# A hybrid decoder trunk: sliding-window scores folded into one 128x128 block per head, and the running sums of both rates from four products

## The chip, the cores and the metric

One core of a Trainium2 chip. Five engines run their own instruction queues in order and meet by semaphores: TensorE (PE, with its weight loads as PEld), VectorE (DVE), ScalarE (ACT), GpSimd (POOL) and SyncE (SP, which here only issues loads). The metric is the device time of one execution in microseconds (us).

## The reference, cut to what matters

Two layers over 256 tokens of width 1024. Each layer normalises the stream, projects it once, runs three token mixers beside each other, gates and merges them, and adds the result to the stream.

```python
proj = einsum('bsd,de->bse', rms_norm(x, norm_w), w_in)
y_a = mamba2_branch(...)           # running sum of dt * a per head, over 128-token chunks
y_b = sliding_window_branch(...)   # 16 query heads, 4 key heads, window 128, a sink logit per head
y_c = forgetting_attention_branch(...)  # running sum of log_sigmoid(f) per head over all 256 tokens
x = x + einsum(merged, w_out)
...
diff = qi + blk - sj                       # qi: query in its block of 128, sj: key in two blocks
band = (diff >= 0) & (diff < SWA_WINDOW)   # window 128
scores = where(band & (key_pos >= 0), scores, -inf)
probs = softmax(concatenate([scores, sink]))[..., :-1]
```

With a window of 128 and blocks of 128, a query at place i of its block sees keys 0..i of its own block and keys i+1..127 of the block before: two triangles that fill one 128x128 square. The first block has no block before it.

## The kernel before, in words

All products of the stream with weights are made in fp32 out of rounded pieces: ScalarE writes the rounded weights (`hi`, L291), VectorE the rest (`lo`, L292), and TensorE multiplies both. SyncE loads the weights; `feed` and `release` (from L404) keep a few split pieces ahead of TensorE, and a piece that TensorE has used frees the place for the next one. So the splits on ScalarE and VectorE are paced by TensorE, and run some us ahead of it.

TensorE's order is fixed by a planner in the file (L100 to L175): each step of work adds its own cost to a clock, and helper tasks (attention, scan, norms) are generators that `yield` a delay after which `pump` may put their next piece between the dense products. The constants at L25 to L33 are these delays (`D_SOFT` behind the softmax, `D_SOFT2` between two batches of transposes, `D_EVAC` behind the evictions, `D_CUM` behind the rates). The order on VectorE, ScalarE and GpSimd is made by a scheduler that knows the tiles.

PSUM has eight banks. Three of them (`pmm`, tag `mm`) take the dense products; five (`pmx`, tag `mx`, L78) are a rotating pool for all that is small: scores, transposes, products with values, running sums, scan products, norm sums. In the pool each request is a tile of its own of one bank.

`attn_quad` (L593) handles four heads. It is used by eight quads of the sliding window (four in each layer, `swa_quad`, L686) and eight of the forgetting attention (`fox_quad`, L976). Its steps: (1) scores of four heads into four `mx` banks, in each 128 columns for the first block of queries and 256 for the second; (2) for each head and block one VectorE instruction that adds a mask or bias, scales and takes the row's minimum (L615), and one ScalarE exponential with its row sum (L621); the sink's share of the sum (L625 to L628); the reciprocal (L630) and the scaling (L633); (3) after `D_SOFT`, twelve 128x128 transposes on TensorE through three `mx` banks (L650), each bank copied out by ScalarE (L652); six of them, then `D_SOFT2`, then six; (4) later, for two quads at once, the products with the values and the gate (`values`, L673, the multiplications at L676).

`decay_logits` (L714) works out the two rates, 16 heads each, and after `D_CUM` their running sums: two products for `acum` (tokens on partitions), two for the scan's rate and three for the forgetting rate (heads on partitions), in three `mx` banks, then one write to DRAM (`cumd`), from which later steps read rows broadcast to all partitions.

`ssd_group` (L805, four in each layer) transposes its inputs through two `mx` banks (L815), each read by VectorE (L817), makes decay blocks (L830, L832), multiplies them by one bank of products (L845) and puts the scan's products into another bank (L851 to L858). `group_norm` (L902) uses `mx` for row sums and scales (L909, L940). The transposes of the stream between layers (`to_hT`, `mT`) use it too.

Of the kernel before, what the change touches and what calls it, by code (L numbers as in the profile page):

```python
# [16 lines left out]
P = 128  # L17
# [30 lines left out]
def hybrid_trunk(  # L48
# [28 lines left out]

    def pmx():  # L78
        return PS("mx", 5)
# [105 lines left out]
    for j in range(2):  # L185
# [17 lines left out]
    wmask = T("wmask", [P, 2 * P])  # L203
    nc.gpsimd.memset(wmask, 0.0)
    nc.gpsimd.affine_select(out=wmask[:, P:2 * P], in_=wmask[:, P:2 * P],
                            compare_op=ALU.is_ge, fill=NEG, base=0,
                            pattern=[[-1, P]], channel_multiplier=1)
    nc.gpsimd.affine_select(out=wmask[:, 0:P], in_=wmask[:, 0:P],
                            compare_op=ALU.is_ge, fill=NEG, base=-1,
                            pattern=[[1, P]], channel_multiplier=-1)  # L210
# [376 lines left out]
    def attn_quad(y, last, products, biases, nsink, v, vcols, sz, gated, scored=lambda: None):  # L587
# [14 lines left out]
        scs = [pmx() for _ in range(4)]  # L602

        def score(p, i, b):
            return scs[2 * p + i][:, b * P:P + 2 * P * b]

        products(score)
        for p in range(2):
            pp = pps[p]
            ps_ = slice(4 * p, 4 * p + 4)  # L610
            ns = None if nsink is None else nsink(p)
            for i in range(2):
                for b, sl in blocks:
                    e = 4 * p + 2 * i + b
                    nc.vector.tensor_tensor_reduce(  # L615
                        out=pp[:, i, sl], in0=score(p, i, b), in1=biases(p, i, b), scale=-0.125,
                        scalar=1.0e30 if ns is None else ns[:, i:i + 1],
                        op0=ALU.add, op1=ALU.min, accum_out=nm[:, e:e + 1])
                for b, sl in blocks:
                    e = 4 * p + 2 * i + b  # L620
                    act(pp[:, i, sl], pp[:, i, sl], AF.Exp, scale=-1.0, bias=nm[:, e:e + 1],  # L621
                        accum_out=sums[:, e:e + 1])
            if nsink is not None:
                es = T("es", [P, 4], bufs=2)
                tt(es.rearrange("p (i b) -> p i b", i=2), nm[:, ps_].rearrange("p (i b) -> p i b", i=2),  # L625
                   bc(ns, 2, 2), op=ALU.subtract)
                act(es, es, AF.Exp)
                tt(sums[:, ps_], sums[:, ps_], es, op=ALU.add)  # L628
            rs = T("rsum", [P, 4], bufs=4)
            nc.vector.reciprocal(rs, sums[:, ps_])  # L630
            for i in range(2):
                for b, sl in blocks:
                    ts(pp[:, i, sl], pp[:, i, sl], rs[:, 2 * i + b:2 * i + b + 1], 0.5,  # L633
                       op0=ALU.mult, op1=ALU.mult)
        yield D_SOFT
        scored()

        order = [(0, 0), (0, 1), (1, 0), (1, 1), (0, 2), (1, 2),
                 (2, 0), (2, 1), (2, 2), (3, 0), (3, 1), (3, 2)]
        at = {hb: (n // 4, n % 4 * P) for n, hb in enumerate(order)}  # L640
        pTs = []
        for n, (h, b) in enumerate(order):
            if n == 6:
                yield D_SOFT2
            if n % 4 == 0:
                pt = pmx()
            transpose(pt[:, n % 4 * P:(n % 4 + 1) * P], pps[h // 2][:, h % 2, b * P:(b + 1) * P], ident)
            if n % 4 == 3:
                if n == 3:
                    two = T("L4", [P, 2, 512])  # L650
                pT = T("L2", [P, 512]) if n == 11 else two[:, n // 4, :]
                act(pT, pt, AF.Copy)  # L652
                pTs.append(pT)
# [3 lines left out]
        def products_with_values(bank):  # L657
            py = bank()
            for p in range(2):
                for b, o in ((0, 0), (1, P)):  # L660
                    for i in range(2):
                        n, c = at[2 * p + i, 2 * b]
                        mm(py[64 * i:64 * i + 64, S * p + o:S * p + S], v[:, b, vcols(p, i)],
                           pTs[n][:, c:c + S - o], start=(b == 0), stop=(b == 1))
            return py
# [3 lines left out]
        if len(pair) == 2:  # L669
            quads = pair[:]  # L670
            pair.clear()

            def values():  # L673
                for py, (_, _, own) in zip([f(bank) for (_, f, _), bank in zip(quads, (pmx, pmm))], quads):
                    o = own()
                    tt(o, py.rearrange("p (u s) -> p u s", u=2), o, op=ALU.mult)  # L676
            if not last:
                y.values.append(None)
            gates = lambda: all(g() for g, _, _ in quads)
            yield Half(gates) if last else gates  # L680
            if last:
                values()
            else:
                y.values[0] = values

    def swa_quad(y, g, q):  # L686
        yield lambda: 1 in y.sz

        def products(score):
# [8 lines left out]
            y, g == 3, products, lambda p, i, b: wmask[:, P:2 * P] if b == 0 else wmask,  # L698
            lambda p: y.nsink[:, 4 * g + 2 * p:4 * g + 2 * p + 2], y.bv,
            lambda p, i: slice(64 * g, 64 * g + 64),  # L700
            lambda: y.sz[1][:, 2 * g:2 * g + 2, :], lambda: (1, 2 * g + 1) in y.zdone)
# [12 lines left out]
    def decay_logits(y):  # L714
# [21 lines left out]
        lf = T("lf", [P, 2, 16])  # L736
# [5 lines left out]
        ts(lf, lf, 2.0, None, op0=ALU.mult)  # L742
        da = T("da", [P, 2, 16])
        tt(da, y.dt, bc(y.nega, 1, 2), op=ALU.mult)
# [15 lines left out]
        mm(pf[0:16, P:S], lf[:, 1, :], tri, start=False, stop=True)  # L760
        act(cum[:, 1, :], pf[0:16, 0:S], AF.Copy, scale=-8.0)
        y.cumd = dr.tile([16, 2, S], F32, name=f"cumd{y.l}", tag=f"cumd{y.l}")
        nc.scalar.dma_start(y.cumd, cum)
# [40 lines left out]
    def ssd_group(y, g):  # L804
# [3 lines left out]
        nc.scalar.dma_start(bcg, y.cumd[4 * g:4 * g + 4, 0, :].partition_broadcast(P))  # L808
# [169 lines left out]
    def fox_quad(y, j):  # L978
# [3 lines left out]
        for p in range(2):  # L982
            bias = T("bias", [P, 2, 3 * P])
            nc.scalar.dma_start(bias[:, :, P:3 * P],
                                y.cumd[2 * (j + p):2 * (j + p) + 2, 1, :].partition_broadcast(P))
# [528 lines left out]
```

## Time and profile before

| | before |
|---|---|
| median of 3 runs | 820.89 us (820.74 to 822.0) |
| the profiled execution, its own time | 820.72 us |
| its span, first to last instruction | 819.0 us |
| DVE, ACT and POOL busy | 671.5, 547.6 and 172.6 us |
| TensorE records | 5242 matmuls, 5242 weight loads |
| HBM read | 154.63 MB, 191 GB/s over the span |

The page gives busy time by engine, a row of digits for 40 slices of the span, the chain of work that ended last (followed back from the last instruction to what released each step) and groups of instructions, written as out<-in by tile names. A timeline lists instructions in order of time, equal neighbours merged: start, length, engine, line, shapes, count. A matmul's length holds its way through the array, and the next one starts before it ends, so what TensorE gives to a matmul is read from start to start. An fp32 matmul has two records.

### The profile page before, as it was taken

How to read it: one execution, taken by the hardware profiler on the slowest of the kernel's cores; microseconds unless marked ns; L12 is line 12 of the kernel's file. 1: busy time of each engine (PE TensorE's matmuls, PEld its weight loads, DVE VectorE, ACT ScalarE, POOL GpSimd, SP SyncE). 2: the span in 40 equal slices, each digit the busy share in tenths (PEclk: the TensorE clock that was granted, in tenths of full speed). 3: DMA queues.
4: the chain of work that ended last, by engine and by line, in shares of the span. 5: the costliest groups of instructions: out<-in, count | busy, mean ns of one | idle time of the engine just before them, and what ended most of it. 6: DMA issues, size and time to landing. Idle time of an engine off the chain costs nothing.

```text
span 819.0 us, 15070 instructions
## 1 busy us (share of the span) xinstructions
PE 808.4 (99%) x5242; PEld 721.2 (88%) x5242; DVE 671.5 (82%) x1468; ACT 547.6 (67%) x1186; POOL 172.6 (21%) x232
## 2 busy tenths in 40 slices
PE   8999999999999999999999999999999999999996
PEld 8998988888888988888999898889888889888896
DVE  6879899888998787965786989988899878787665
ACT  7777878775776767543666777886567767684452
POOL 3066113130210001030005621314004210102100
PEclk9999999999999999999999999999999999999999
DMA  9897869797865554866689787869868565467632
GB/s 312 278 261 193 211 187 256 190 233 214 232 206 157 180 168 148 276 208 205 221 265 265 186 222 206 228 179 259 243 206 231 155 181 163 137 208 265 206 104 77
DMA packets 141653, 170.35 MB, mean 208 GB/s; under 512 B 9314, under 2 KB 110298, under 8 KB 141578
## 3 DMA queue, kind: packets, MB, share of 16 engines
q1 hardware_dynamic: 114960, 140.53, 54.8%
q0 software_dynamic: 12928, 12.63, 9.5%
q10 hardware_dynamic: 13690, 16.24, 6.5%
q8 instruction: 41, 0.67, 0.3%
q14 instruction: 34, 0.28, 0.1%
HBM read 154.63 MB, written 2.16 MB: 191 GB/s over the span
## 4 chain that ended last, share of the span: by engine, by line
PE 85%; DVE 4%; DMA 4%; ACT 4%; issue 2%; POOL 0%; SPq 0%; ACTq 0%; DVEq 0%; POOLq 0%
PE mm L106 75%; PE mx L106 7%; PE mx L110 3%; DMA L<-cumd 2%; DVE lo L292 1%; ACT hi L291 1%; DVE L L781 1%; ACT pp L621 1%; DMA L<-L 1%; DMA raw<-in_w_in_dram 1%; DMA bias<-cumd 1%; ACT L L778 0%; ACT L L490 0%; DVE L L830 0%; POOL bias L991 0%
## 5 line engine op out<-in xcount | busy, mean ns | idle before, releaser
L292 DVE TENSOR_TENSOR lo<-raw,hi 128x1024 fp32r<-128x1024 f32 (+2 forms) x276 | 310.5, 1144 | 53.2 <-ACT hi L291 50.5
L106 PE MATMUL mm<-L,hi 128*128 128x512 f32 x1056 | 353.2, 386 | 0.0
L106 PE MATMUL mm<-hi,L 128*128 128x512 f32 (+2 forms) x1232 | 323.3, 351 | 0.1
L291 ACT ACTIVATE hi<-raw 128x1024 fp32r<-128x1024 f32 (+2 forms) x276 | 263.9, 981 | 57.2 <-PE mm L106 45.2
L106 PE MATMUL mm<-L,lo 128*128 128x256 f32 x1056 | 266.6, 273 | 0.0
L106 PEld LDWEIGHTS mm<-hi,L 128*128 128x128 f32 x1232 | 216.9, 190 | 24.1 <-issue 1.3
L106 PEld LDWEIGHTS mm<-L,hi 128*128 128x128 f32 x1056 | 194.5, 190 | 26.4 <-issue 3.2
L106 PE MATMUL mm<-lo,L 128*128 128x512 f32 (+2 forms) x616 | 213.8, 349 | 1.8 <-DVE lo L292 1.8
L106 PEld LDWEIGHTS mm<-L,lo 128*128 128x128 f32 x1056 | 202.1, 191 | 5.5
L106 PEld LDWEIGHTS mm<-lo,L 128*128 128x128 f32 x616 | 116.3, 190 | 14.1 <-DVE lo L292 2.6
L492 POOL DMA_DIRECT2D L<-L x68 | 59.4, 925 | 184.5 <-ACT L L491 151.3
L621 ACT ACTIVATE pp<-pp,nm 128x128 f32<-128x128 f32 (+1 forms) x128 | 56.5, 442 | 30.8 <-DVE nm L615 30.7
L991 POOL TENSOR_SCALAR_AFFINE_SELECT bias<-bias 128x128 f32<-128x128 f32 x64 | 34.6, 592 | 93.5 <-DMA bias<-cumd 92.7
L781 DVE SCALAR_TENSOR_TENSOR L<-L,vec,L 128x255 f32<-128x255 f32 (+2 forms) x96 | 46.2, 481 | 2.2 <-ACT L L778 0.5
L490 ACT ACTIVATE L<-mm 128x256 f32<-128x256 f32 x84 | 31.6, 376 | 15.9 <-PE mm L106 14.2
L1025 ACT ACTIVATE L<-L 128x512 f32<-128x512 f32 x24 | 15.1, 629 | 31.6 <-DVE L L1022 27.2
L633 DVE TENSOR_SCALAR pp<-pp,rsum 128x128 f32<-128x128 f32 (+1 forms) x128 | 32.5, 319 | 0.5
L492 POOL DMA_DIRECT2D qt<-L x16 | 14.5, 990 | 81.9 <-ACT qt L491 40.4
L877 DVE SCALAR_TENSOR_TENSOR L<-L,L 128x256 f32<-128x256 f32 x48 | 21.4, 449 | 8.6 <-ACT L L876 8.3
L652 ACT ACTIVATE L<-mx 128x512 f32<-128x512 f32 x48 | 26.8, 595 | 1.5 <-PE mx L110 1.5
L1070 POOL TENSOR_TENSOR L<-L,L 128x512 f32<-128x512 f32 x8 | 12.8, 1598 | 68.4 <-DVE L L1069 68.4
L912 POOL TENSOR_TENSOR sm<-sm,mhalf 128x4 f32<-128x4 f32 x8 | 8.1, 1019 | 90.5 <-DVE sm L909 90.5
(197 smaller groups left out, 841.8 us busy)
## 6 DMA issues: line engine op xcount, KB each, us to landing
raw<-in_w_in_dram SPq DMA_DIRECT2D x191, 512.0 KB, 4.7
raw<-in_w_proj_dram SPq DMA_DIRECT2D x48, 512.0 KB, 5.3
L<-L POOLq DMA_DIRECT2D x72, 128.0 KB, 5.0
raw<-in_w_out_dram SPq DMA_DIRECT2D x16, 512.0 KB, 5.1
bias<-cumd ACTq DMA_DIRECT2D x16, 256.0 KB, 3.4
L<-cumd ACTq DMA_DIRECT2D x8, 512.0 KB, 5.9
L<-in_gate_bias_dram ACTq DMA_DIRECT2D x12, 256.0 KB, 5.9
qt<-L POOLq DMA_DIRECT2D x16, 128.0 KB, 5.6
```

The source lines that it names most:

```text
L106: nc.tensor.matmul(o, a, b, **kw)
L110: nc.tensor.transpose(o, a, i)
L291: keep(act)(hi, src, AF.Copy)
L292: keep(tt)(lo, src, hi.bitcast(F32), op=ALU.subtract)
L490: act(halves(lo), ordered(p[:, S:2 * S]), AF.Copy)
L492: nc.gpsimd.dma_start(out, lo, accum_op=ALU.add)
L621: act(pp[:, i, sl], pp[:, i, sl], AF.Exp, scale=-1.0, bias=nm[:, e:e + 1], accum_out=sums[:, e:e + 1])
L633: ts(pp[:, i, sl], pp[:, i, sl], rs[:, 2 * i + b:2 * i + b + 1], 0.5, op0=ALU.mult, op1=ALU.mult)
L652: act(pT, pt, AF.Copy)
L781: stt(a[:, s:S], x_[:, 0:S - s], y.vec[:, 16 * j + u:16 * j + u + 1], a[:, s:S], op0=ALU.mult, op1=ALU.add)
L877: stt(o, th, 1.0, o, op0=ALU.add, op1=ALU.mult)
L991: nc.gpsimd.affine_select(out=bias[:, i, dst], in_=bias[:, i, src], compare_op=ALU.is_ge, fill=NEG, base=0, pattern=[[-1, P]], channel_mul ...
```

## The change

Three things are changed.

**Banks.** The five `mx` banks become one tile of five banks, `banks`, and `pmx` hands out its slices in turn. `pmx4` hands out four neighbouring banks as one slice, 0 to 3 or 1 to 4, whichever leaves out the end bank that was used later. Every quad takes its scores through `pmx4`, so that one VectorE instruction can span four heads.

**Window quads.** For each block of queries, a predicated copy puts, in the square of keys, the later keys' places over: for the first block by -1e30, for the second by the scores of the block before. Then one maximum over four heads, the sink, and four exponentials that read PSUM; the scaling is one multiplication by a broadcast. Eight transposes are made in place of twelve, through two banks. The first bank is copied out by ScalarE; the second, which holds both triangles, is read twice by VectorE, each time by a product with a 0/1 triangle. The factor 0.5 moves to the gate. The delay behind the softmax is `D_FOLD` = 8.0.

**Running sums.** Both rates stand beside each other in `rates`. One product gives `acum`; two of 32 rows and one of 16 rows give the sums of both rates, the two halves of the tokens on different partitions of one bank. One copy takes them out, and two writes go to DRAM. `D_CUM` goes from 12 to 17.

The diff, cut to its core:

```diff
-D_GN1, D_GN2, D_CUM, D_H, D_M = 8.0, 13.5, 12.0, (4.8, 6.4), 5.0
+D_GN1, D_GN2, D_CUM, D_H, D_M = 8.0, 13.5, 17.0, (4.8, 6.4), 5.0
+D_FOLD = 8.0
...
+    banks = ps.tile([P, 5, 512], F32, tag="mx", name="mx", bufs=1)
+    oldest = list(range(5))
     def pmx():
-        return PS("mx", 5)
+        oldest.append(oldest.pop(0))
+        return banks[:, oldest[-1], :]
+    def pmx4():
+        a = 0 if oldest.index(4) > oldest.index(0) else 1
+        for i in range(a, a + 4):
+            oldest.append(oldest.pop(oldest.index(i)))
+        return banks[:, a:a + 4, :]
...
-        scs = [pmx() for _ in range(4)]
+        sc = pmx4()
...
+        for b in range(2) if window else ():
+            own = sc[:, :, 2 * b * P:2 * b * P + P]
+            hs = slice(4 * b, 4 * b + 4)
+            nc.vector.copy_predicated(own, bc(later, 1, 4).bitcast(mybir.dt.uint32),
+                                      sc[:, :, P:2 * P] if b else bc(least.to_broadcast([P, P]), 1, 4))
+            nc.vector.tensor_reduce(nm[:, hs], own, axis=mybir.AxisListType.X, op=ALU.max)
+            stt(nm[:, hs], nm[:, hs], -0.125, nsink, op0=ALU.mult, op1=ALU.min)
+            for h in range(4):
+                e = 4 * b + h
+                act(pps[b][:, h // 2, h % 2 * P:h % 2 * P + P], own[:, h, :], AF.Exp, scale=0.125, bias=nm[:, e:e + 1],
+                    accum_out=sums[:, e:e + 1])
+            es = T("es", [P, 4], bufs=2)
+            tt(es, nm[:, hs], nsink, op=ALU.subtract)
+            act(es, es, AF.Exp)
+            tt(sums[:, hs], sums[:, hs], es, op=ALU.add)
+            rs = T("rsum", [P, 4], bufs=4)
+            nc.vector.reciprocal(rs, sums[:, hs])
+            tt(of_heads(b), of_heads(b), bc(rs.rearrange("p (i j) -> p i j", i=2), 3, P), op=ALU.mult)
...
-        yield D_SOFT
+        yield D_FOLD if window else D_SOFT
...
+        if window:
+            first, both = T("L4", [P, 2, 512]), T("L2", [P, 512])
+            for b in range(2):
+                if b == 1:
+                    yield D_SOFT2
                 pt = pmx()
+                for h in range(4):
+                    transpose(pt[:, h * P:(h + 1) * P], pps[b][:, h // 2, h % 2 * P:h % 2 * P + P], ident)
+                ptv = pt.rearrange("p (h q) -> p h q", h=4)
+                if b == 0:
+                    act(first[:, 0, :], pt, AF.Copy)
+                else:
+                    tt(first[:, 1, :].rearrange("p (h q) -> p h q", h=4), ptv, bc(other, 1, 4), op=ALU.mult)
+                    tt(both.rearrange("p (h q) -> p h q", h=4), ptv, bc(tri, 1, 4), op=ALU.mult)
...
         pa = pmx()
-        for c in range(2):
-            mm(pa[:, 16 * c:16 * c + 16], tri, da[:, c, :], start=True, stop=True)
+        mm(pa[:, 0:32], tri, rates[:, :, 1, :], start=True, stop=True)
         y.acum = T("acum", [P, 2, 16])
         act(y.acum, pa[:, 0:32].rearrange("p (t c) -> p t c", t=2), AF.Copy)
-        cum = T("L2", [16, 2, S])
-        pr = pmx()
+        pc = pmx()
         for c in range(2):
-            mm(pr[0:16, c * P:(c + 1) * P], da[:, c, :], tri, start=True, stop=True)
-        act(cum[:, 0, :], pr[0:16, 0:S], AF.Copy)
-        pf = pmx()
-        mm(pf[0:16, 0:P], lf[:, 0, :], tri, start=True, stop=True)
-        mm(pf[0:16, P:S], lf[:, 0, :], ones, start=True, stop=False)
-        mm(pf[0:16, P:S], lf[:, 1, :], tri, start=False, stop=True)
-        act(cum[:, 1, :], pf[0:16, 0:S], AF.Copy, scale=-8.0)
-        nc.scalar.dma_start(y.cumd, cum)
+            mm(pc[32 - 32 * c:64 - 32 * c, 0:P], rates[:, c, :, :].rearrange("p w c -> p (w c)"), tri,
+               start=True, stop=(c == 0))
+        mm(pc[0:16, 0:P], rates[:, 0, 0, :], ones, start=False, stop=True)
+        cum = T("L1", [64, P])
+        act(cum, pc[0:64, 0:P], AF.Copy)
+        for c in range(2):
+            nc.scalar.dma_start(y.cumd[:, :, c * P:(c + 1) * P].rearrange("w c s -> (w c) s"),
+                                cum[32 - 32 * c:64 - 32 * c, :])
```

The values' products read `first` (both parts, 256 columns) for the first block of keys and `both` for the second; the masks `later`, `other` and `least` replace `wmask`. The fox quads keep their softmax and their twelve transposes.

More of the change, by code (lines that the diff above doesn't have):

```diff
@@ L201, in hybrid_trunk @@
     ones = onesr.bitcast(F32)
[L203 to L210, printed above, removed]
+    later, other = T("later", [P, P]), T("other", [P, P])
+    for m, way in ((later, 1), (other, -1)):
+        nc.gpsimd.memset(m, 1.0)
+        nc.gpsimd.affine_select(out=m, in_=m, compare_op=ALU.is_ge, fill=0.0, base=-1,
+                                pattern=[[way, P]], channel_multiplier=-way)
+    least = T("least", [P, 1])
+    nc.gpsimd.memset(least, NEG)
     mhalf = T("mhalf", [P, 8])
@@ L585, in u_bq, with attn_quad @@
         return rotated(y, done)
-    def attn_quad(y, last, products, biases, nsink, v, vcols, sz, gated, scored=lambda: None):
+    def attn_quad(y, last, products, biases, nsink, v, vcols, sz, gated, scored=lambda: None, window=False):
         yield Half("pp")
@@ L661, in products_with_values @@
                     for i in range(2):
[L662 to L664 removed]
+                        h = 2 * p + i
+                        if window:
+                            m = both[:, h * P:(h + 1) * P] if b else first[:, :, h * P:(h + 1) * P]
+                        else:
+                            n, c = at[h, 2 * b]
+                            m = pTs[n][:, c:c + S - o]
+                        mm(py[64 * i:64 * i + 64, S * p + o:S * p + S], v[:, b, vcols(p, i)], m,
+                           start=(b == 0), stop=(b == 1))
             return py
@@ L697, in swa_quad @@
         yield from attn_quad(
-            y, g == 3, products, lambda p, i, b: wmask[:, P:2 * P] if b == 0 else wmask,
-            lambda p: y.nsink[:, 4 * g + 2 * p:4 * g + 2 * p + 2], y.bv,
+            y, g == 3, products, None, y.nsink[:, 4 * g:4 * g + 4], y.bv,
             lambda p, i: slice(64 * g, 64 * g + 64),
-            lambda: y.sz[1][:, 2 * g:2 * g + 2, :], lambda: (1, 2 * g + 1) in y.zdone)
+            lambda: y.sz[1][:, 2 * g:2 * g + 2, :], lambda: (1, 2 * g + 1) in y.zdone, window=True)
     def logits(y, t, i, p):
```

67 lines of the change are left out of this document (34 added, 33 removed).

## The prediction

> **What bounds the kernel now.** First the page: its head, the busy shares and the chain.
>
> ```profile
> span 819.0 us, 15070 instructions
> ...
> PE 808.4 (99%) x5242; PEld 721.2 (88%) x5242; DVE 671.5 (82%) x1468; ACT 547.6 (67%) x1186; POOL 172.6 (21%) x232
> ...
> PE 85%; DVE 4%; DMA 4%; ACT 4%; issue 2%; POOL 0%; SPq 0%; ACTq 0%; DVEq 0%; POOLq 0%
> ```
>
> TensorE is busy 99% and is 85% of the chain. Next, what TensorE waited for (us in all, times, longest), and the windows view of a stretch of layer 0 with window quads (us, then PE, PEld, DVE, ACT and POOL busy, clock, DMA share, GB/s).
>
> ```profile
> PE mm L106 <- DVE lo L292: 1.8, 2, 1.2
> PE mx L110 <- POOL ident masks.py:199: 1.5, 1, 1.5
> PE mx L106 <- ACT hi L1389: 0.5, 2, 0.3
> ```
>
> ```profile
> 68.00:160.00 92.00, 92.00 (x688) 82.60 (x689) 84.19 (x233) 75.22 (x199) 25.65 (x32) 1.00 0.75 200
> ```
>
> All waits of TensorE come to 3.8 us. In that stretch it has no idle time, while VectorE, at 84.19 of 92.00, and ScalarE, at 75.22, keep up. So the time is the sum of TensorE's work, plus whatever makes TensorE stand; work on the other two counts only if TensorE comes to wait for it. No wait above is for a reader of an `mx` bank: five banks in turn were enough.
>
> **The change, part by part.**
>
> *TensorE's work.* From the timeline (start, length):
>
> ```profile
> 75.81 0.82 PE L110 MATMUL mx<-ident,pp 128*128 128x128 f32 x6
> 76.39 0.46 PE L106 MATMUL mm<-L,hi 128*128 128x512 f32 x1
> ...
> 112.47 1.59 PE L106 MATMUL mx<-L,qt 32*128 32x128 f32 x32
> ...
> 116.71 0.51 PE L106 MATMUL mx<-da,tri 128*128 128x16 f32 x4
> 117.16 0.61 PE L106 MATMUL mx<-tri,da 128*16 128x128 f32 x4
> 117.60 0.38 PE L106 MATMUL mx<-tri,lf 128*16 128x128 f32 x2
> ...
> 118.35 0.48 PE L106 MATMUL mm<-L,hi 128*128 128x512 f32 x1
> ```
>
> From start to start, six transposes take 0.58, so 0.097 each. Eight quads drop four each: 32 x 0.097 = 3.1 us. The sums took 118.35 - 116.71 = 1.64, of which 0.1 is the next matmul's start. One product of the `acum` kind goes (0.45 / 2 = 0.22), and of five 128-column products (0.44 / 2 = 0.22 each) three stay: 0.65 a layer, 1.3 in both. Together -4.4 us.
>
> *Work on VectorE and ScalarE.*
>
> ```profile
> 115.41 0.68 DVE L676 TENSOR_TENSOR L<-mm,L 128x512 f32<-128x512 f32 x1
> 116.01 0.34 DVE L615 CUSTOM_DVE_ANT_0 pp<-mx,wmask,nsink 128x128 f32<-128x128 f32 x1
> ```
>
> ```profile
> 118.49 0.48 DVE L615 CUSTOM_DVE_ANT_0 pp<-mx,wmask,nsink 128x256 f32<-128x256 f32 x1
> ```
>
> ```profile
> 116.40 0.40 ACT L621 ACTIVATE pp<-pp,nm 128x128 f32<-128x128 f32 x1 [4.90 <-DVE nm L615]
> ```
>
> ```profile
> L633 DVE TENSOR_SCALAR pp<-pp,rsum 128x128 f32<-128x128 f32 (+1 forms) x128 | 32.5, 319 | 0.5
> L652 ACT ACTIVATE L<-mx 128x512 f32<-128x512 f32 x48 | 26.8, 595 | 1.5 <-PE mx L110 1.5
> ```
>
> VectorE gives up, per window quad, 4 x (0.34 + 0.48) at L615 and 8 x 0.32 at L633: 5.8. It gets two predicated copies, two maxima, two scalings and two triangle products, all of 512 columns. Before has no predicated copy and no such reduction; the nearest row of that size reading PSUM is L676 at 0.68 (0.60 to the next start), so 8 x 0.68 and 0.8 of small ones: 6.2. A copy might cost half (0.34) or twice (1.36) of that; I take the row (it moves E, below, by -0.7 to +1.4, inside its ends). So +0.4 per quad; ScalarE saves some 1.3 (four exponentials of 256 columns become 128, two copies go). TensorE's 92 us hide this in that stretch; without the cover eight quads would cost 3.2.
>
> *DMA.* The tile view of `cumd` and of the bias give the first readers (shortest, median and longest ns, first and last start).
>
> ```profile
> L808 ACTq DMA_DIRECT2D L<-cumd x8: 366/372/378, 158.6 to 593.0; - x8
> ```
>
> ```profile
> L615 DVE CUSTOM_DVE_ANT_0 pp<-mx,bias x64: 263/343/422, 213.4 to 686.2; 128x128 f32<-128x128 f32 x32, 128x256 f32<-128x256 f32 x32
> ```
>
> The sums leave by two writes on ScalarE's queue instead of one, and `D_CUM` is 17 for 12. The scan reads them back 42 us behind the sums, and the fox bias made of them is used 97 us behind: that distance hides both.
>
> *New waits.* `banks` is one tile now. The instruction order of the changed program names each wait: a TensorE write into any `mx` bank waits for the last reader of every earlier `mx` bank, not only of its own. VectorE and ScalarE serve their queues in order, and everything dense on TensorE stands behind the waiting matmul. Where much TensorE work lies between, this costs nothing. I went through all places where little or none lies between. A hand-over costs at least the reader's time and 0.05 (116.35 to 116.40 above), and the 0.24 that a transpose's way through the array adds (0.82 - 0.58).
>
> ```profile
> 227.29 0.82 PE L110 MATMUL mx<-ident,pp 128*128 128x128 f32 x6
> ```
>
> ```profile
> 229.83 1.07 ACT L652 ACTIVATE L<-mx 128x512 f32<-128x512 f32 x2
> ```
>
> ```profile
> L817 DVE TENSOR_TENSOR L<-mx,dt 128x256 f32<-128x256 f32 x16 | 6.3, 415 | 0.0
> ```
>
> ```profile
> 172.79 0.60 PE L110 MATMUL mx<-ident,L 128*128 128x128 f32 x4
> ```
>
> ```profile
> 177.29 0.42 DVE L817 TENSOR_TENSOR L<-mx,dt 128x256 f32<-128x256 f32 x1
> 234.90 0.28 DVE L615 CUSTOM_DVE_ANT_0 pp<-mx,bias 128x128 f32<-128x128 f32 x1
> ...
> 237.21 0.39 DVE L615 CUSTOM_DVE_ANT_0 pp<-mx,bias 128x256 f32<-128x256 f32 x1
> ```
>
> ```profile
> 208.01 1.88 DVE L845 TENSOR_TENSOR L<-L,mx 128x512 f32<-128x512 f32 x3
> ```
>
> ```profile
> L292 DVE TENSOR_TENSOR lo<-raw,hi 128x1024 fp32r<-128x1024 f32 (+2 forms) x276 | 310.5, 1144 | 53.2 <-ACT hi L291 50.5
> ```
>
> - **A, 17 places**: fox transposes into a second bank wait for ScalarE's copy of the first, fed just before. 0.60 + 0.24 + two hand-overs: 1.0 each. Low 0.65 (copy and one hand-over), high 2.3 (the copies at 229.83, the first done at some 230.4, against 228.11, the end of the transposes).
> - **B, 8 places**: the second transposes of `ssd_group` wait for L817 of the first. 0.42 + 0.24 + 0.1, and half a split (L292, 1.14) in front: 1.2. Low 0.55, high 4.3 (177.71 against 173.39).
> - **C, 3 places** in layer 0: scan products right behind fox scores wait for all eight L615, 234.90 to 237.60: 2.7. Low 2.2 (8 x 0.28), high 4.9 (two splits more). Two more in layer 1 have 2.6 us of TensorE's work between: 0.4.
> - **D, 2 places**: fox transposes right behind the bank that three L845 read: 1.88 and 0.3, so 2.2. Low 1.9, high 3.3 (a split more).
> - **E, 2 places**: the running sums still follow the third window quad's scores; from their end, 112.47 + 1.59 = 114.06, to the sums at 116.71 are 2.65 us. Now exponentials read PSUM, so the sums wait for the whole softmax: copy and maximum 1.2, 0.2, four exponentials 1.6; copy and maximum of the second block 1.2, its copy behind the first block's exponentials (same banks); other work on VectorE 1.2; four exponentials 1.6: 7.0, begun half a split (0.6) after the scores. 7.6 - 2.65 = 5.0, and 0.5 as the second bank of the sums waits for the copy of the first: 5.5. Low 3.4, as the row below ends at 120.13, 3.4 behind 116.71; high 7.8 (two splits more).
> - **F, small ones**: rows below; transposes at the start of the program and between the layers, four scores behind the values' L676, and the norm's L909 and L940: 8 in all, from 3 to 16.
>
> ```profile
> 119.94 0.19 ACT L621 ACTIVATION_READ_ACCUMULATOR pp<-pp,nm 128x1 f32 x1
> ```
>
> ```profile
> L909 DVE TENSOR_SCALAR sm<-mx 128x4 f32<-128x4 f32 x8 | 1.1, 155 | 0.0
> L940 DVE SCALAR_TENSOR_TENSOR L<-L,vec,mx 128x256 f32<-128x256 f32 x16 | 6.9, 474 | 0.0
> ```
>
> The sum: 17 + 9.6 + 8.9 + 4.4 + 11 + 8 = 58.9. From it go the 4.4 of work and the 1.8 that TensorE waits for splits now, since each stand lets the splits run ahead. 820.7 + 58.9 - 6.2 = 873.4 against the profiled execution, which is 0.2 under the median: **873 us**. All lows together are 35.7, so 850; all highs 126, but they can't come together, as a standing TensorE lets both readers' queues empty.
>
> **The rivals.**
>
> *Only the banks really held cost.* If the waits across banks are answered in time, as a reader that has nothing ahead of it would do, only E stays, where a softmax really holds four banks: 820.7 - 4.4 + 11 = 827. Against it: L817 came 3.9 us behind its transposes in a queue that is busy 84 of 92 us. [...]
>
> *Faster: only the work counts.* The mechanism is the 32 transposes and six products that go: 820.7 - 4.4 = 816.3. It decides if all waits together stay under 4.4 us, which over the 34 places of A to F's larger kinds is 0.13 us each. The shortest reader of a bank in the rows is L909 at 0.155; the readers of A and B take 0.42 and 0.60. Also against it are the two real holds of E.
>
> *The clock falls in the gaps.* The trace has one hint, at its start, behind the 1.5 us wait for `ident`.
>
> ```profile
> 1.52 1.76 PE L110 MATMUL mx<-ident 128*128 128x128 f32 x7 [1.52 <-POOL ident masks.py:199]
> 3.21 2.38 PE L110 MATMUL mx<-ident,L 8*128 8x8 f32 x9
> 5.38 1.38 PE L110 MATMUL mx<-ident 128*128 128x128 f32 x10
> 6.70 0.49 PE L106 MATMUL mx<-hi,L 128*128 128x256 f32 x2
> ```
>
> ```profile
> 0.00:4.00 4.00, 2.35 (x10) 1.93 (x11) 0.23 (x2) 1.90 (x3) 2.68 (x16) 1.00 0.47 145
> ```
>
> The first transposes come every 0.24 us, those from 5.38 every 0.13, though the granted clock reads 1.00 in both. If each of the two gaps of E brings 4 us at half pace, that is 2 us lost per gap, 877; if the many gaps of A to D keep TensorE at half pace for a fifteenth of its 808 us (54 us), 27 us more are lost: 904. [...]
>
> **How the numbers follow.** Forecast 0.80; only the held banks 0.09; faster 0.04; clock 0.07. The range is 848 to 905: 850 less the error of the work term, up to the clock's upper end, which also covers B's queueing at half its excess (12) and A's (11) on 873. It leaves out 827 and 816 and a little of both tails, 0.2. About 0.2% (1.6 us) is what a measurement can tell from no change. Faster by more 0.04, within 0.01, slower 0.95.
>
> **What would show it.** TensorE's waits should list, new, ScalarE's fox copies (A, some 17 us), VectorE at L817's place (B, 10), fox minima (C, 9), and ScalarE's exponentials or the `acum` copy before the sums (E, 11); TensorE's busy time should fall by some 4, and its wait for `lo` should go. In a fox quad there should be a gap of 1 us inside each batch of six transposes. If TensorE's waits stay under 5 us, the waits across banks are harmless and I am wrong from A on. If its busy time grows by over 10, the clock is at work. If waits for `lo` or `hi` grow by several us instead, VectorE has become the bound and my 0.4 per quad was wrong.

## The result, and the profile after

The changed kernel takes 928.81 us (median of 4 runs, 925.75 to 929.04) against 821.19 us for the kernel before: 1.130 times as long, 95% interval 1.1275 to 1.1326. Forecast were 873 us and a range up to 905. The direction and the place were right, the size was half of what came.

The page after: span, busy shares, the granted clock in 40 slices, the chain.

```profile
span 926.9 us, 14870 instructions
...
PE 840.6 (91%) x5198; PEld 739.0 (80%) x5198; DVE 681.9 (74%) x1356; ACT 542.2 (58%) x1168; POOL 162.4 (18%) x234
...
PEclk9999999999899988899999999899999999899999
...
PE 69%; DVE 14%; ACT 9%; issue 4%; DMA 3%; POOL 0%; ACTq 0%; DVEq 0%; POOLq 0%
```

Three things are to be seen. TensorE's records show 44 matmuls fewer, and yet it is busy 32 us longer. Its share of the chain falls from 85% to 69%, and what it lost went to VectorE and ScalarE, though VectorE's own busy time rose by only 10 us. And the clock row, all nines before, now has eights; this is the row before:

```profile
PEclk9999999999999999999999999999999999999999
```

What TensorE waited for (us in all, times, longest), cut below 1.9 us:

```profile
PE mx L122 <- ACT L L695: 14.4, 16, 2.1
PE mx L118 <- DVE nm L649: 11.1, 3, 5.1
PE mx L122 <- DVE L L868: 10.4, 9, 3.6
PE mx L118 <- ACT pp L634: 9.3, 2, 4.6
PE mx L118 <- DVE L L991: 5.5, 2, 2.9
PE mx L118 <- issue: 5.3, 2, 2.7
PE mx L122 <- DVE L L896: 5.1, 2, 2.6
PE mx L122 <- DVE sm L960: 4.6, 2, 2.3
PE mx L122 <- DVE sm L257: 2.9, 1, 2.9
PE mx L122 <- DVE L L1427: 2.4, 3, 0.8
PE mx L122 <- ACT pp L634: 1.9, 2, 0.9
```

Every new line waits on the `mx` side, and the wait for `lo` is gone. L695 is the copy behind the forgetting quads' transposes (A of the prediction), L868 the scan's inputs (B), L649 the minima (C), L896 the decay blocks (D), L634 the window's exponentials (E). The timeline of TensorE at the running sums shows a stand and what follows it:

```profile
126.69 0.38 PE L118 MATMUL mm<-L,hi 128*128 128x512 f32 x1
131.71 0.41 PE L118 MATMUL mx<-rates,tri 128*128 128x32 f32 x2 [4.63 <-ACT pp L634]
132.40 0.64 PE L118 MATMUL mx<-tri,rates 128*32 128x128 f32 x4 [0.29 <-ACT acum L801]
...
134.41 0.63 PE L118 MATMUL mm<-L,hi 128*128 128x512 f32 x1
134.84 0.42 PE L118 MATMUL mm<-L,lo 128*128 128x256 f32 x1
```

Behind the 4.63 us the dense products go at half pace: an `hi` product takes 0.43 to the next start (134.41 to 134.84), where it took 0.22 before (119.87 to 120.09):

```profile
119.87 0.38 PE L106 MATMUL mm<-L,hi 128*128 128x512 f32 x1
120.09 0.27 PE L106 MATMUL mm<-L,lo 128*128 128x256 f32 x1
```

The windows view around the longest stand, cut every 3.4 us, has the granted clock in the column behind POOL:

```profile
231.20:234.60 3.40, 0.00 (x0) 0.00 (x0) 3.40 (x9) 1.62 (x4) 0.86 (x1) 1.00 0.99 246
234.60:238.00 3.40, 1.73 (x16) 1.73 (x18) 2.84 (x18) 3.25 (x16) 0.00 (x0) 0.50 0.84 284
238.00:241.40 3.40, 3.40 (x20) 2.79 (x17) 1.95 (x7) 0.00 (x0) 1.16 (x5) 0.50 0.45 124
241.40:244.80 3.40, 2.88 (x19) 2.44 (x19) 1.46 (x5) 0.80 (x2) 0.84 (x4) 0.99 0.00 0
```

**The account.** The span grew by 926.9 - 819.0 = 107.9 us. Taken from the records of all matmuls: TensorE stands (no matmul is under way) 80.0 us instead of 4.3 (+75.7). The clock is at 0.50 in 12 pieces of 3.41 or 6.83 us, 61.4 us together, in 4.9 of which TensorE stands; the other 56.5 count half, so 28.3 us are lost. 51 stands of over 0.3 us, 48 more than before, each show once more the part of a matmul's length that in a stream lies behind the next one's start (0.38 - 0.22 = 0.16 us; it is called the way through the array here): some 7.7 by estimate. The work saved is -4.4, also an estimate. Together 107.3.

One loss is not in it. The trace's clock records begin 12.76 us after the start of the span, in the trace of before 5.62 us, and the time ahead of them is counted as full clock. But the matmuls there go at half pace; ten transposes take some 2.4 us, where the ten at 5.38 in the kernel before took 1.38:

```profile
7.73 2.40 PE L122 MATMUL mx<-ident 128*128 128x128 f32 x10 [0.79 <-DVE L L1427]
```

Of these 7.1 us more, TensorE works 6.1, so about 3 us more are lost. With them the terms come to 110.4, 2.5 more than the span grew: the two estimates are off by that much together, and which of them is open.

### The profile page after: what moved, and what is told of

Same layout as the page of the kernel before. It is cut to its first block, busy times and chain, and to the rows that moved or that the text cites. A ratio compares the mean times of both kernels' runs of the same rounds, so it can differ in the third digit from the quotient of the medians.

```text
span 926.9 us, 14870 instructions
## 1 busy us (share of the span) xinstructions
PE 840.6 (91%) x5198; PEld 739.0 (80%) x5198; DVE 681.9 (74%) x1356; ACT 542.2 (58%) x1168; POOL 162.4 (18%) x234
## 4 chain that ended last, share of the span: by engine, by line
PE 69%; DVE 14%; ACT 9%; issue 4%; DMA 3%; POOL 0%; ACTq 0%; DVEq 0%; POOLq 0%
PE mm L118 60%; PE mx L118 5%; PE mx L122 4%; DVE lo L303 4%; ACT hi L302 3%; DMA L<-cumd 2%; DVE L L832 2%; ACT pp L634 1%; ACT L L695 1%; DVE pp L649 1%; ACT pp L655 1%; DMA raw<-in_w_in_dram 1%; DVE mx L628 1%; DVE nm L630 1%; DVE L L896 1%
## 5 line engine op out<-in xcount | busy, mean ns | idle before, releaser
L118 PE MATMUL mm<-L,hi 128*128 128x512 f32 x1056 | 366.4, 397 | 0.0
L118 PE MATMUL mm<-hi,L 128*128 128x512 f32 (+2 forms) x1232 | 329.2, 356 | 0.0
L118 PE MATMUL mm<-L,lo 128*128 128x256 f32 x1056 | 272.7, 279 | 0.0
L118 PEld LDWEIGHTS mm<-hi,L 128*128 128x128 f32 x1232 | 221.9, 194 | 24.6 <-issue 1.2
L118 PEld LDWEIGHTS mm<-L,hi 128*128 128x128 f32 x1056 | 201.1, 196 | 29.0 <-issue 5.0
L118 PE MATMUL mm<-lo,L 128*128 128x512 f32 (+2 forms) x616 | 217.2, 354 | 0.0
L118 PEld LDWEIGHTS mm<-L,lo 128*128 128x128 f32 x1056 | 209.0, 198 | 6.0
L118 PEld LDWEIGHTS mm<-lo,L 128*128 128x128 f32 x616 | 118.5, 193 | 12.3
L122 PE MATMUL mx<-ident,pp 128*128 128x128 f32 x160 | 28.1, 292 | 26.5 <-ACT L L695 14.4
L1042 POOL TENSOR_SCALAR_AFFINE_SELECT bias<-bias 128x128 f32<-128x128 f32 x64 | 25.6, 442 | 121.3 <-DMA bias<-cumd 90.6
L122 PEld LDWEIGHTS mx<-ident,pp 128*128 128x128 f32 x160 | 19.2, 145 | 32.9 <-ACT L L695 18.3
L634 ACT ACTIVATE pp<-mx,nm 128x128 f32<-128x128 f32 x64 | 22.6, 365 | 29.2 <-DVE nm L631 29.2
L655 ACT ACTIVATE pp<-pp,nm 128x128 f32<-128x128 f32 x64 | 28.2, 441 | 15.2 <-DVE nm L649 15.2
L122 PE MATMUL mx<-ident,L 128*128 128x128 f32 (+2 forms) x101 | 18.7, 294 | 16.2 <-DVE L L868 9.9
```

The costliest lines, as they stand in the source:

```text
L118: nc.tensor.matmul(o, a, b, **kw)
L122: nc.tensor.transpose(o, a, i)
L634: act(pps[b][:, h // 2, h % 2 * P:h % 2 * P + P], own[:, h, :], AF.Exp, scale=0.125, bias=nm[:, e:e + 1], accum_out=sums[:, e:e + 1])
L1042: nc.gpsimd.affine_select(out=bias[:, i, dst], in_=bias[:, i, src], compare_op=ALU.is_ge, fill=NEG, base=0, pattern=[[-1, P]], channel_mul ...
```

## Experiments

Where experiments are timed, the kernel before ran beside them at medians of 820.95 to 821.9 us; "lost to the clock" is counted as above.

### The tile alone

The kernel before, with only this:

```diff
-    def pmx():
-        return PS("mx", 5)
+    banks = ps.tile([P, 5, 512], F32, tag="mx", name="mx", bufs=1)
+    oldest = list(range(5))
+    def pmx():
+        oldest.append(oldest.pop(0))
+        return banks[:, oldest[-1], :]
```

> The kernel before with one edit: the five mx banks are one tile, handed out in turn; softmax, transposes and sums are those of before. Theory (the waits across banks come from the one tile, and gaps of some us then halve the clock for 3.4 or 6.8 us): nearly all waits of the changed kernel stay, less the 11 us in front of the sums, plus some 14 us as window quads again turn through three banks: TensorE stands 75 to 90 us, clock pieces at half speed cost 20 to 35 us more, 915 to 940 us in all. Rival (the fold itself, with its copies and maxima on VectorE, makes TensorE wait): without the fold the time stays within 815 to 830 us.

Measured: 952.33 us, 1.160 times the kernel before (1.156 to 1.164). This is above the range of 915 to 940: TensorE stands 95.9 us, where 75 to 90 were expected; 30.0 are lost to the clock, inside the 20 to 35. Its first waits:

```profile
PE mx L114 <- ACT L L656: 43.4, 32, 3.4
PE mx L114 <- DVE L L821: 14.0, 9, 4.0
PE mx L110 <- DVE nm L619: 9.9, 5, 4.4
```

The tile alone is worse than the whole change, as 16 quads, not 8, now turn through three banks in batches of six (32 waits for the copy, two a quad). No operation of the fold is in this kernel, so the rival, 815 to 830 us without the fold, falls.

### Separate banks, with the fold and the sums

The changed kernel, with `pmx` of before, and the two four-head instructions made one head at a time:

```diff
-        sc = pmx4()
+        sc = [pmx() for _ in range(4)]
...
-            nc.vector.copy_predicated(own, bc(later, 1, 4).bitcast(mybir.dt.uint32),
-                                      sc[:, :, P:2 * P] if b else bc(least.to_broadcast([P, P]), 1, 4))
-            nc.vector.tensor_reduce(nm[:, hs], own, axis=mybir.AxisListType.X, op=ALU.max)
+            for h in range(4):
+                nc.vector.copy_predicated(own[h], later.bitcast(mybir.dt.uint32),
+                                          sc[h][:, P:2 * P] if b else least.to_broadcast([P, P]))
+                nc.vector.tensor_reduce(nm[:, 4 * b + h:4 * b + h + 1], own[h], axis=mybir.AxisListType.X, op=ALU.max)
```

> The changed kernel with the five banks as tiles of their own; the predicated copy and the maximum are made for each head by itself, all else as changed. Theory: the waits across banks go, 75 of 80 us of TensorE's standing with them, and the clock stays at 1.00 but for the sums: their second bank is one that the third window quad still holds, so up to 5 us a layer stay, with 1 to 3 us of half clock; 818 to 832 us. Rival (the fold makes the waits): over 890 us. A third possibility: the 12 more instructions on VectorE per quad make it the bound, seen as waits for lo, 835 to 850 us.

Measured: 836.44 us, 1.0185 (1.0165 to 1.0204). The waits, largest first:

```profile
PE mx L107 <- ACT acum L791: 13.3, 2, 6.7
...
PE mx L107 <- DVE rates L785: 1.2, 2, 0.6
```

The waits across banks are gone, 92 of the 108 us with them. One remains, twice: the second bank of the sums is the first of the third quad, whose exponentials read it (the profile names ScalarE's last instruction ahead, the `acum` copy). That stand was put at up to 5 us and is 6.65, so the time lies 4 us above my range. Account: +14.4 us standing, +4.1 clock, -4.4 work, and the way through the array.

### The fold alone and the sums alone

The fold on separate banks with the sums of before, and the sums (with `D_CUM` 17) on the kernel before:

> The fold alone, on banks of their own (copy and maximum per head), with the running sums of before. Theory: TensorE's work falls by 3.1 us; two of the three banks of the sums are banks that the third quad holds, up to 5 us a layer: 818 to 832 us, and within 2 us of the run with both parts. Rival (the fold makes the waits): over 890 us.

> The running sums from four products alone, placed by 17, on the kernel before. Theory: 1.3 us of TensorE's work go, nothing waits: 819 to 821 us. Rival (the later place makes the scan or the forgetting bias late): over 823 us, with a wait of TensorE behind rows read from cumd.

Measured: the fold alone 839.11 us (1.0193 to 1.0241), above its range of 818 to 832, with the same kind of stand before the sums (12.9 us in both layers); the sums alone 823.88 us (1.0026 to 1.0051), slower where 0 to 2 us less were expected. In the second, not the scan is late (no wait for rows of `cumd`), but the last window quad: VectorE begins its first L615 at 143.10 in layer 0, against 139.69 before, and TensorE's transposes wait for the scaling, 1.08 us in layer 0 and 0.81 in layer 1. The rival had the time right, but neither it nor the theory this cause. The steps ahead of it on VectorE come in the same order as before, 3.4 us later.

### The sums out of the held bank

Two ways on separate banks: all products of the sums into one bank (the fifth), or the sums placed by 25.

```diff
         pa = pmx()
+        pc = pa[:, P:2 * P]
         mm(pa[:, 0:32], tri, rates[:, :, 1, :], start=True, stop=True)
-        y.acum = T("acum", [P, 2, 16])
-        act(y.acum, pa[:, 0:32].rearrange("p (t c) -> p t c", t=2), AF.Copy)
-        pc = pmx()
...
         mm(pc[0:16, 0:P], rates[:, 0, 0, :], ones, start=False, stop=True)
+        y.acum = T("acum", [P, 2, 16])
+        act(y.acum, pa[:, 0:32].rearrange("p (t c) -> p t c", t=2), AF.Copy)
```

> The changed kernel on separate banks (copy and maximum per head), with all four products of the sums into one bank, the fifth, which no quad holds. Theory: the two stands of 6.65 us before the second bank go, and the half clock behind them (6.8 and 10.2 us at half speed, 8.5 us); what is left is the 4.4 us of work saved less 1 to 2 us of small waits: 816 to 819 us, faster than before by 0.3 to 0.6%. Rival (the fold loads VectorE so that TensorE waits for splits): over 823 us.

> The changed kernel on separate banks (copy and maximum per head), with the sums placed by 25 instead of 17, behind the softmax that holds the second bank, and the banks as changed. Theory: the same gain by another way: 816 to 820 us. Rival (later sums make the scan's row loads late): TensorE waits behind rows from cumd, over 823 us.

Measured: 825.08 us (1.0041 to 1.0066) and 825.48 us (1.0041 to 1.0072). The stand before the sums and the half clock are gone in both (clock pieces: none). That is worth 11 us, where 17 to 20 were expected, and neither beats the kernel before: both ranges missed. The waits of the first:

```profile
PE mx L111 <- DVE pp L632: 1.6, 1, 1.6
PE mx L111 <- ACT L L798: 1.6, 2, 0.8
...
PE mm L107 <- DVE L L1061: 1.5, 2, 0.8
PE mx L107 <- ACT hi L1428: 1.3, 1, 1.3
PE mx L107 <- DVE rates L785: 1.2, 2, 0.6
PE mm L107 <- DVE u L750: 1.0, 3, 0.4
```

TensorE stands 11.4 us, 7.1 more than before, in many waits of about a us, more than half of it behind VectorE. These outweigh the work saved. In all runs with the fold on separate banks the copies and maxima are made head by head, 12 more instructions on VectorE for each window quad, so the small waits are those of the fold in this form.

### Less work on VectorE, and longer delays

On the kernel with the sums in one bank, first without the two triangle products (the expectation says what that leaves out), then with `D_FOLD` 10 and `D_CUM` 22.

```diff
...
-                    tt(first[:, 1, :].rearrange("p (h q) -> p h q", h=4), ptv, bc(other, 1, 4), op=ALU.mult)
-                    tt(both.rearrange("p (h q) -> p h q", h=4), ptv, bc(tri, 1, 4), op=ALU.mult)
+                    act(first[:, 1, :], pt, AF.Copy)
...
```

> The run on separate banks with the sums in one bank (825.1 us), where the two triangle products on VectorE are left out: ScalarE copies the second transposed bank once, and both blocks of keys use that copy, so the later keys of both blocks enter with wrong weights. Per window quad VectorE loses 1.37 us, ScalarE gets 0.6. Theory (the small waits of TensorE behind VectorE, some 7 us, come from the 10 us of work that the fold adds there, so they ate the 4.4 us): the waits fall by half or more, 818 to 821 us. Rival (they come from where the pieces stand in the queue, not from the load): 823 to 826 us, no change.

> The run on separate banks with the sums in one bank, with the delay behind the folded softmax at 10 for 8 and that of the sums at 22 for 17. Theory (the waits for the scaling and for the rates, 1.6 and 1.2 us, are delays set too short for the longer VectorE chain): 820 to 823 us, about the kernel before. Rival (the later pieces push others into waits): 824 us or more.

Measured: 823.45 us (1.0007 to 1.0035) and 828.91 us (1.0074 to 1.0099). Taking 7 us of busy time from VectorE (681.1 to 674.1) takes 3 of the 7 us of extra standing (11.4 to 8.4), just short of half, and the time lies inside the rival's range: load may be one part and place in the queue another; this run does not part them. Longer delays made it worse, against a range of 820 to 823: the two waits they aimed at went, and TensorE waits 4.5 us for the window's minima instead, with two clock pieces. This one change of the delays did not remove the fold's own cost.

### The sums alone, in one bank

> The kernel before with the running sums by four products in one bank, at the delay 12 of before. Theory: 1.3 us of TensorE's work and two ScalarE instructions go per pair of layers, and the softmax is not pushed as it was at 17: 819 to 820.5 us, faster by 0.1 to 0.25%. Rival (any change of the order on VectorE and ScalarE costs a us or two): 822 to 824 us as with the sums at 17.

Measured: 819.04 us, 0.9962 of the kernel before (0.995 to 0.9974). Busy shares and waits:

```profile
PE 807.2 (99%) x5230; PEld 720.9 (88%) x5230; DVE 672.2 (82%) x1468; ACT 546.6 (67%) x1184; POOL 168.6 (21%) x232
```

```profile
PE mm L106 <- DVE lo L292: 1.7, 2, 1.0
PE mx L110 <- POOL ident masks.py:199: 1.5, 1, 1.5
PE mx L110 <- DMA L<-in_x_dram: 0.5, 1, 0.5
```

The waits are nearly those of before, and TensorE's busy time is 1.2 us less. Beside the kernel before (821.9 us) the gain is 2.9 us, more than that and more than the 0.1 to 0.25% expected; where the rest comes from was not traced. This is the part of the change that pays, and the fastest version of all that ran.

### Two stands mended inside the one tile

The changed kernel with `D_CUM` 25, and the changed kernel with the forgetting quads' transposes in three batches of four, a bank each:

```diff
-                if n == 6:
+                if n in (4, 8):
                     yield D_SOFT2
```

> The changed kernel, its one tile kept, with the sums placed by 25 instead of 17. Theory: the 11.2 us before the sums go, and the half clock behind them (3.4 and 6.8 us at half speed, 5 us); all other waits stay: 908 to 916 us. Rival (a stand that goes at the sums comes back at the next write into the tile): 925 us or more.

> The changed kernel, its one tile kept; the forgetting quads' twelve transposes go in three batches of four, one bank each, with the delay of 3 between them, instead of two of six. Theory (a wait across banks costs only where no TensorE work lies between): the 14.4 us behind ScalarE's copies go, with two or three of the twelve half-clock windows: 906 to 915 us. Rival (a stand that goes comes back at the next write): 922 us or more.

Measured: 922.5 us (917.15 to 927.03) and 906.56 us (905.9 to 908.08). With the sums later, the 9.3 us behind the exponentials go, but two new waits of 1.6 come where the transposed bank is copied:

```profile
PE mx L118 <- ACT L L676: 3.2, 2, 1.6
```

TensorE still stands 75.4 us, and in the profiled execution 32.0 us were lost to the clock, more than the 28.3 of the changed kernel: what was won by standing less went there. That execution, 927.03 us, was the longest of its four; the median is 6.3 us below the changed kernel. The range was missed, the rival is half right: a stand that goes comes back in part at the next write, since some other reader of the tile is late there. With three batches the largest line of the changed kernel, the transposes' 16 waits for the copies (L122, 14.4 us), is gone. But other products (L118) now wait seven times for the same copies, where in the changed kernel they did once, for 1.1 us:

```profile
PE mx L118 <- ACT L L695: 7.7, 7, 1.8
```

In all, standing falls by 11.3 us (80.0 to 68.7) and the loss to the clock by 9.0 (28.3 to 19.3), together 20.3 of the 21.9 us by which the span is shorter (926.9 to 905.0). So the transposes' wait across banks became free once dense work lay between, as the prediction had it, and the rival is half right here too: about half of it came back at later writes. In this run a stand saved paid nearly twice, once by itself and once by the clock; with the sums later it did not.

### The clock

First the kernel on separate banks with its stand of 6.65 us filled:

```diff
         mm(pa[:, 0:32], tri, rates[:, :, 1, :], start=True, stop=True)
+        for i in range(50):
+            nc.tensor.transpose(pa[:, P:2 * P], ident, ident)
```

> The run with separate banks and sums by 17 (836 us), with 50 transposes of the identity, which nobody reads, put on TensorE between the first product of the sums and the second, where it stood 6.65 us. Theory (a 3.4 us window in which TensorE stands over 2 us halves the next one): the 50 transposes take 5 us of the stand, the rest of it is under 2 us, the clock stays at 1.00, and the time falls by 8 us to 826 to 830 us though work was added. Rival (the stand alone costs, the clock is only a mark): 836 us as before, or 5 us more.

Measured: 834.66 us (1.0153 to 1.0181), above the range of 826 to 830. Without the filler it was 836.44 (1.0165 to 1.0204): the intervals overlap, so these 1.8 us are not clear of noise. Its timeline:

```profile
120.23 5.66 PE L791 MATMUL mx<-ident 128*128 128x128 f32 x50
127.98 0.41 PE L107 MATMUL mx<-tri,rates 128*32 128x128 f32 x4 [2.09 <-ACT pp L624]
128.22 0.38 PE L107 MATMUL mx<-ones,rates 128*16 128x128 f32 x2
```

The products behind go at full pace (0.24 and 0.32 from start to start, 0.44 and 0.56 without the filler), so 11 us of matmuls were added in the two layers and the run was no longer. The gain of 8 us did not come, as I had counted all 17.1 us at half clock as time in which TensorE works. In 8.8 of them TensorE stood, so only 4.1 could be won; and another stand of 2.65 us cost 1.7 by a half piece of its own. That run moved two things at once, so the clock was tried on the kernel before, with stands put behind its dense products, 12 long ones or 24 short ones (6 fills in place of 14):

```diff
+    def stand():
+        p = pmm()
+        nc.tensor.transpose(p[:, 0:P], still, ident)
+        for _ in range(14):
+            nc.gpsimd.memset(still, 1.0)
+        nc.tensor.transpose(p[:, P:2 * P], still, ident)
...
```

> The kernel before with 12 stands of TensorE put between dense products far from other small work: a transpose reads a tile, GpSimd fills that tile 14 times (0.2 us each), a second transpose reads it again. Nothing reads the result. Theory (a window of 3.4 us in which TensorE stands over 2 us halves the next one): each stand is about 3 us, some 36 us in all; about 9 of 12 fall so that one window holds over 2 us, each then loses 1.7 to 3.4 us: 870 to 880 us, with 8 to 11 pieces at half clock. Rival (only the whole standing time counts for the clock, not how it is cut): the same number of half pieces as with twice as many stands of half the length.

> The kernel before with 24 stands of half the length (GpSimd fills the tile 6 times), twice as many places. Theory: each stand is about 1.5 us, 36 us in all as with the long ones, but no window holds 2 us, so the clock stays at 1.00: 855 to 862 us, some 15 us less than with the 12 long stands. Rival: half clock as with the long stands, 870 us or more.

Measured: 897.35 us (1.0883 to 1.0948) and 882.24 us (1.0716 to 1.076). Both are above their ranges, as most stands are 3.80 and 1.69 us, not 3 and 1.5. What TensorE waited for, long and short:

```profile
PE mm L1486 <- POOL still L1485: 47.3, 12, 5.7
```

```profile
PE mm L1486 <- POOL still L1485: 41.7, 23, 2.8
PE mm L1486 <- DVE lo L292: 4.3, 1, 4.3
```

The sum of standing is the same (51.7 and 50.5 us over the span). The long stands make 10 pieces at half clock, 19.9 us lost; the short ones 2, 4.7 us lost, both behind stands of 2.0 us or more. The clock's difference of 15.2 us is larger than that of the two profiled spans, 10.4 (891.5 and 881.1), since the short form has 12 stands more, with their 24 transposes and the way through the array each time. So for the clock it mattered here how the standing is cut, not its sum over the run. Two of the twelve long stands made no half piece, and the windows view shows why. First one of these, then one that did, cut on the grid of 3.41 us on which all half pieces begin:

```profile
393.60:397.00 3.40, 1.46 (x10) 1.07 (x8) 1.39 (x2) 1.12 (x2) 1.44 (x7) 1.00 0.86 293
397.00:400.40 3.40, 1.54 (x8) 1.39 (x9) 0.00 (x0) 0.05 (x1) 1.44 (x7) 1.00 0.02 7
400.40:403.80 3.40, 3.40 (x18) 2.97 (x17) 2.29 (x2) 2.92 (x3) 0.00 (x0) 1.00 0.09 5
410.70:414.10 3.40, 0.65 (x4) 0.60 (x5) 0.37 (x1) 0.00 (x0) 2.12 (x11) 1.00 0.08 28
414.10:417.50 3.40, 3.40 (x10) 2.67 (x9) 0.00 (x0) 1.06 (x1) 0.00 (x0) 0.50 0.00 0
417.50:420.90 3.40, 3.40 (x19) 2.98 (x18) 0.14 (x1) 0.00 (x0) 0.00 (x0) 1.00 0.00 0
```

Both are some 3.8 us long. The first is cut by the grid into 1.94 and 1.86, and the clock stays; the second has 2.75 in one window, and the next runs at half.

## Why the prediction was wrong, by its own steps

- **What bounds the kernel** held: TensorE's work and its standing, at the clock that it had, make the account above to within 2.5 us.
- **TensorE's work** (-4.4) held as far as it can be read: the sums' 1.3 were 1.2 of busy time in the run with the sums alone; the fold's 3.1 can't be read by themselves.
- **VectorE's and ScalarE's work hidden** held in the changed kernel and not beyond it. +0.4 us a quad was counted, 3.2 in all; the lengths of all VectorE's instructions together, without its waits for semaphores, fell by 4.7 (764.8 to 760.1), but its busy time rose by 10.4, as fewer of them overlap (93.3 us of overlap before, 78.2 now). Copies and maxima came at 0.69 to 0.75 us each, priced at 0.68. TensorE's standing covers that. On separate banks the cover is thin: 7.1 us of small waits, more than half behind VectorE, ate the work saved (there the instructions for each head bring the lengths to 774.4, with the busy time at 681.1).
- **The waits across banks** were the right mechanism, shown by the tile alone (952 us) and by separate banks (836 us). A to E were forecast at 17 + 9.6 + 8.9 + 4.4 + 11 = 50.9 and came to 14.4 + 10.4 + 11.1 + 5.1 + 9.9 = 50.9. That the two totals agree is luck, as errors cancel: copies and sums were priced too high, minima too low. At the longest of these, 5.14 us, VectorE did two splits and two smaller steps between the scores and the first minimum.
- **F failed**: 8 us, with an end at 16, and 27.2 came (L991 5.5, scores behind the values 5.3, L960 5.4, and more at the start and between the layers). I priced the reader (155 and 474 ns) and not the queue ahead of it. The scores behind the values waited 2.7 us from 120.0, as VectorE came to the first bank of values only at 121.87, 3.2 us after it was written.
- **The clock failed as a step of the forecast.** It stood as a rival at 7%, priced at up to 31 us; 28.3 came. The sign named for it came, as TensorE's busy time grew by 32 us (over 10 was the sign). But the price's 54 us at half pace were assumed, not worked out from rows; that 56.5 us of work at half clock came is luck. No run shows the 4 us at half pace that were priced for each gap of E: in the changed kernel these two gaps, of 4.63 us each, were followed by pieces of 3.41 and 6.83 us. The chance was too low, as the upper price needed gaps shorter than those of E to bring the half clock, and gaps of 2.1 to 2.9 us made eight of the twelve pieces. The hint quoted for it, transposes 0.24 us apart at the start and 0.13 later, does not show how long a gap must be: the clock of 1.00 that was read there stands for no record at all (the records begin at 5.62 us), and the half pace there need not come from the wait of 1.5 us.
- **The way through the array** (some 7.7 us over 48 stands) was in the prices of A, B and D; in this account it stands apart from the waits.

So two steps failed: F was put at 8 us where 27.2 came, and the clock was left out of the sum where it took 28.3. These 19.2 and 28.3 are 47.5 of the 107.9 - 52.7 = 55.2 us by which the forecast missed. The rest is the way through the array (7.7 by estimate) and the start (about 3), less the 2.5 by which the account is too high and small things. The rival with only the held banks (827) fits the kernel on separate banks by its mechanism (only the stand before the sums is left, 13.3 us for the 11 it had; 836 us) and not the change; the rival with only the work (816) is answered by the run with the sums in one bank: even with no wait across banks the fold, made head by head, did not pay.

What stays open: why the fold's 7 us of small waits arise, since taking VectorE's work away removed less than half of them, and whether four-head instructions would do better if each bank were tracked by itself. That was not tried.

## What to carry to other kernels

Before joining buffers into one tile so that one instruction can span them, list who writes and who reads each of them: here every write then waited for the last reader of all (the tile alone took 952.33 us, 1.160 times the kernel before), and it cost wherever the writer had no other work between. Price such a wait by the queue ahead of the reader, not by the reader. And on an engine that is busy 99%, standing had a second price here, in the clock: 24 short stands lost 4.7 us to it, 12 long ones of nearly the same sum 19.9 us.

## What the runs showed of the hardware

The half clock came in whole windows of 3.41 us on a fixed grid: the twelve pieces of the changed kernel are 3.41 or 6.83 us long, and their starts lie whole multiples of 3.413 us apart. In that kernel all 12 windows at full clock in which TensorE, before its last matmul, stood 2.0 us or more were followed by one at 0.50, and none of the 19 with 0.9 to 2.0 us of standing was. Over ten runs here (the changed kernel and nine experiments), all 66 windows at full clock in which TensorE stood 2.0 us or more were followed by one at 0.50; of some 115 windows with 0.9 to 2.0 us of standing, four were (at about 1.55 to 1.96). So standing in some 60% of a window, 2.0 of 3.41 us, was enough here. In the changed kernel, stands of 2.1 to 2.9 us made eight of the twelve half pieces, two of them (before 258.5 and 354.1) only together with a second stand in the same window.
